# A WKV recurrence on one core: another order of the small state work and of the first loads

## The chip, the cores and the metric

The kernel runs on one core of a Trainium2 chip. A core has a matrix engine (PE, TensorE), a vector engine (DVE, VectorE), a scalar engine (ACT, ScalarE) and a general engine (POOL, GpSimd); SP (SyncE) here only issues transfers. Each engine takes its own instructions strictly in order and waits for the others through semaphores. Sixteen DMA engines move data between the chip's memory (HBM) and the core; the transfers that POOL issues stand under q0 in the profile, those of SP under q1. The metric is the device time of one launch in microseconds (us): the median of the executions shown.

## The reference

For each of 16 sequences and each of 256 channels, a running sum with exponential weights over 2048 tokens, kept safe by a running maximum `pp`:

```python
for b in range(batch):                 # 16
    aa, bb, pp = zeros, zeros, full(-1e38)
    for t in range(seq_len):           # 2048
        kk, vv = k[b, t, :], v[b, t, :]
        ww = u + kk
        qq = maximum(pp, ww)
        e1, e2 = exp(pp - qq), exp(ww - qq)
        output[b, t, :] = (e1 * aa + e2 * vv) / (e1 * bb + e2 + 1e-08)
        ww = pp - w + kk
        qq = maximum(ww, kk)
        e1, e2 = exp(ww - qq), exp(kk - qq)
        aa, bb, pp = e1 * aa + e2 * vv, e1 * bb + e2, qq
```

`k`, `v` and the output are 16 x 2048 x 256 in float32, 33.6 MB each; `w` and `u` are rows of 256.

## The kernel before

**Tiling.** The 2048 tokens are cut into a head of 32 (`T0`) and 16 steps of 126 (`TC`). Tokens lie on partitions. A step is worked on in four pairs, each with four sequences (a tile of 128 x 1024 float32, 512 KB, for `k` and one for `v`; the rows beyond 126 belong to the next step). The head fills two pairs of its own, three groups of 32 tokens stacked on 96 partitions, loaded by small transfers, one for each group. All pairs stand in one list: step 0's first two, the two head pairs (numbers 2 and 3), step 0's last two (4 and 5), then four for each step; 66 in all.

**One pair.** `round_k` (DVE, L287) casts `k` into a tile `km` that also holds `w` and `u` in its last rows; `logs` (PE, L303) multiplies it by two constant matrices into `X`, four PSUM banks (all the log weights); `exps` (ACT, L319; L317 in two parts for pairs 0 to 7) makes `ez` of it; `cast_v` (L330 on DVE, L328 on ACT for pairs 2 to 7) and `times_v` (DVE, L338) multiply by `v`; `sums` (PE, L368) adds up the pair's tokens into the step's totals `tot`. Ten slots later (`LAG`; six for a head pair) the pair's output is made: `den` (PE, L514), its logarithm `log_den` (ACT, L523), `invert` one slot later (ACT, L528), and in the slot after that `num` (PE, L536), `mult` (DVE, L544) and `store` (POOL, L564), `num` and `mult` once for each half of the pair. `den` has one PSUM buffer and `num` has one: `num` of the second half cannot start before `mult` of the first half has read the buffer.

**The state.** Between steps a small state is carried: `copy_sums` (ACT) takes the totals, `turn_sums` (PE, L384) transposes them into the buffer of `den`, `split_sums` (DVE, L391, tile `tsum`) takes them from there, and then a dozen instructions on tiles of some 64 columns follow, DVE and ACT by turns: `state_logs`, `state_offset` (tile `S`, L408), `state_near` (L412), `state_weights`, `state_sums` (`tb`, L441), `state_add` (`da`, L446), `state_decay` (`AB`, L452), `inject_logs`, `inject_weights` (`phi`), `carry_weights` (L468), `carries` (`ab`, L475), `turn_carries` (PE, L481, also in the buffer of `den`), and `inject` (DVE, `row`, L486), which ends in four small transfers on SP's queue (L490) that put the carried state into two rows of `ez`. The `den` of the step's pairs needs those rows.

**Order.** One loop (L617 to L674) runs over slots n; slot n works on `exps`, `times_v` and `sums` of pair n, on `round_k`, `cast_v` and `logs` of pair n+1, on the loads of pair n+4 and on the output of older pairs. The order of the calls is kept on every engine, so a call's place in the loop is its place in its engine's queue. The state's work is hung into the loop by name: `small_work(n, "d0")` and so on run what `PLANS` has put there, as (slots after the step's last pair, place, function). The first letter of a place says which engine it is meant for: d for DVE, p for PE, a for ACT. In slot 10 alone (`late`) `den` and `log_den` stand behind `sums`.

**Loads.** Four buffers for each of `k` and `v`. Pairs 0 to 3 are loaded ahead of the loop: the rows of `w` and `u`, then the two first pairs, and then the head's ten small transfers, all on SP's queue; all later loads and the stores are issued by POOL, in order. POOL also makes constant patterns; those for the head (`patterns_for_head`) come after the head's loads, and DVE makes matrices of them (`matrices_for_head`) after the first pair's casts.

Of the kernel before, what the change touches and what calls it, by code (L numbers as in the profile page):

```python
# [22 lines left out]
def kernel(  # L23
# [90 lines left out]
    def load(n):  # L114
        kr = kpool.tile([128, 4, Dm], F32, tag="kr", name="kr")
        vr = vpool.tile([128, 4, Dm], F32, tag="vr", name="vr")
        kr_of[n], vr_of[n] = kr, vr
        c, p = pairs[n]
        if is_head(n):
            if p == 1:  # L120
                K(POOL.memset(kr[64:96, 0:2, :], 0.0))
                K(POOL.memset(vr[64:96, 0:2, :], 0.0))
            for t, x in ((kr, k), (vr, v)):
                for g in range(NG):
                    b = 6 * g + 4 * p
                    e = min(b + 2 * tiles_of(n), B)
                    if b < e:
                        K(SP.dma_start(out=t[g * GB:(g + 1) * GB, 0:e - b, :],
                                        in_=x[b:e, 0:T0, :].rearrange("n t d -> t n d")))
        else:  # L130
            t0 = T0 + c * TC
            r = min(128, T - t0)
            for t, x in ((kr, k), (vr, v)):
                K((SP if n < 2 else POOL).dma_start(  # L134
                    out=t[0:r, :, :], in_=x[4 * p:4 * p + 4, t0:t0 + r, :].rearrange("n t d -> t n d")))
# [71 lines left out]
    K(DVE.scalar_tensor_tensor(NLE[:, TC + 1:128], cc[:, 2:3], -0.5 * HS, cc[:, 4:5], ALU.mult, ALU.add))  # L207
    for n in range(2, AHEAD):
        load(n)
# [8 lines left out]

    OHE, OHV, OHhE, OHhV = [matrix(x, BF16, 56) for x in ("OHE", "OHV", "OHhE", "OHhV")]

# [7 lines left out]

    def patterns_for_head():
        unit(0, NH)  # L230
        unit(1, NH + 1)
        K(POOL.iota(IOh[:, 0:NH], pattern=[[0, NG], [1, GB]], base=0, channel_multiplier=0,
                    allow_small_or_imprecise_dtypes=True))
        K(POOL.memset(OHhE, 0.0))
        K(POOL.memset(OHhV, 0.0))
        for g in range(NG):
            K(POOL.memset(OHhE[g * GB:(g + 1) * GB, 8 + 3 * g:9 + 3 * g], 1.0))
            K(POOL.memset(OHhV[g * GB:(g + 1) * GB, 24 + 3 * g:25 + 3 * g], 1.0))
            select(OHhE[:, 40 + 3 * g:41 + 3 * g], NE, 1.0, NH + g, -1, 1, 0)
# [117 lines left out]
    def sums(n):  # L357
# [5 lines left out]
        for i in range(tiles_of(n)):  # L363
            for q in range(2):
# [211 lines left out]
    def small_work(n, where):  # L576
        for f, args in later.pop((n, where), []):
# [3 lines left out]
        "head": ((1, "a0", copy_sums), (1, "p2", turn_sums), (2, "d0", split_sums), (2, "a1", state_logs),  # L581
                 (3, "a0", state_weights), (3, "d4", state_start)),
# [26 lines left out]
    patterns_for_head()  # L609
# [4 lines left out]
    matrices_for_head()  # L614

    out_at = {n + (LAG - 4 if is_head(n) else LAG): n for n in range(NP)}
    for n in range(NP + LAG + 2):  # L617
# [5 lines left out]
        if n + AHEAD < NP:  # L623
            load(n + AHEAD)
        if live:
            exps(n)
# [14 lines left out]

        late = n == LAG
        if out_q and not late:
# [7 lines left out]
        if out_qp:  # L651
            mult(qp, 0)
            if live:
                num(qp, 1)
# [18 lines left out]
        small_work(n, "d5")  # L673
        small_work(n, "a1")  # L674
# [31 lines left out]
```

## Time and profile before

| what | value |
|---|---|
| median of 13 runs | 331.9 us (325.75 to 337.45) |
| the profiled execution | 331.9 us, of it 330.2 us from its first to its last instruction |
| HBM read and written | 68.10 MB and 34.05 MB |
| POOL issues of loads and stores of 512 KB | 60 stores, 58 loads of `k`, 58 of `v`; median 7.5, 8.3 and 8.7 us from issue to landing |
| state transfers on SP's queue (`ez<-row`) | 64 of 8 KB, median 6.6 us to landing |
| mean granted PE clock | 0.965 of full speed |

By stages, as the stretches of the trace show them: up to about 44 us the pipeline fills (pairs 0 to 9, the head among them); up to about 94 us the first outputs begin; from 94.4 to 285.7 us eleven steps run alike, four pairs in about 17.4 us each; after 291 us the outputs of the last pairs are finished, with one logarithm and one exponential on ACT for each pair, about 2 us.

How to read the lines that follow. A line of busy time gives us and the share of the span for each engine. The rows of digits cut the span into 40 equal slices: a digit is a busy share in tenths. A line of the waits names the engine and line that waited, what it waited for, and then us in total, times, and the longest. A line of the timeline gives start, duration, engine, line, operation and shapes; in brackets stand the engine's idle time before it and what ended that. A line of stretches gives, for each, the busy us of each engine, the granted PE clock, the busy share of the DMA engines and GB/s.

### The profile page before, as it was taken

How to read it: one execution, taken by the hardware profiler on the slowest of the kernel's cores; microseconds unless marked ns; L12 is line 12 of the kernel's file. 1: busy time of each engine (PE TensorE's matmuls, PEld its weight loads, DVE VectorE, ACT ScalarE, POOL GpSimd, SP SyncE). 2: the span in 40 equal slices, each digit the busy share in tenths (PEclk: the TensorE clock that was granted, in tenths of full speed). 3: DMA queues.
4: the chain of work that ended last, by engine and by line, in shares of the span. 5: the costliest groups of instructions: out<-in, count | busy, mean ns of one | idle time of the engine just before them, and what ended most of it. 6: DMA issues, size and time to landing. Idle time of an engine off the chain costs nothing.

```text
span 330.2 us, 3900 instructions
## 1 busy us (share of the span) xinstructions
PE 282.9 (86%) x1116; PEld 130.4 (39%) x1132; DVE 275.7 (84%) x547; ACT 280.5 (85%) x318; POOL 176.0 (53%) x244
## 2 busy tenths in 40 slices
PE   1649795979999999999999999999999999997980
PEld 1214332434444444444444444444444444433430
DVE  4824794697999999999999999999999999997761
ACT  6439784859989898999999998999898989897890
POOL 7328963336446566656555666666564656111431
PEclk9996989599999999999999999999999999999996
DMA  5997699849999999999999999999999999954776
GB/s 174 284 288 247 186 324 325 240 145 329 325 334 355 350 356 357 379 368 354 368 370 378 357 361 370 378 348 355 360 375 362 365 330 323 299 217 134 257 264 180
DMA packets 34071, 102.93 MB, mean 312 GB/s; under 512 B 6610, under 2 KB 9938, under 8 KB 34050
## 3 DMA queue, kind: packets, MB, share of 16 engines
q0 software_dynamic: 27408, 98.75, 87.4%
q1 hardware_dynamic: 6642, 3.94, 4.8%
q8 instruction: 9, 0.15, 0.2%
q14 instruction: 12, 0.10, 0.1%
HBM read 68.10 MB, written 34.05 MB: 309 GB/s over the span
## 4 chain that ended last, share of the span: by engine, by line
PE 37%; DMA 25%; DVE 20%; ACT 10%; issue 5%; SPq 1%; DVEq 0%; POOL 0%; POOLq 0%; ACTq 0%
DMA vr<-in_v_dram 21%; PE num L536 10%; PE tot L368 9%; PE X L303 8%; DVE rd L544 6%; PE den L514 6%; DVE ez L338 5%; DMA ez<-row 5%; DVE vb L330 3%; ACT rd L523 3%; DVE km L287 3%; ACT ez L317 2%; ACT ez L319 2%; PE den L384 2%; ACT vb L328 1%
## 5 line engine op out<-in xcount | busy, mean ns | idle before, releaser
L319 ACT ACTIVATE ez<-X 128x2048 bf16<-128x2048 f32 x58 | 108.8, 1876 | 15.5 <-PE X L303 15.2
L564 POOL DMA_DIRECT2D out_dram<-rd x64 | 50.0, 781 | 120.0 <-issue 76.4
L544 DVE TENSOR_TENSOR rd<-num,rd 128x512 f32<-128x512 f32 (+2 forms) x131 | 88.5, 682 | 9.1 <-ACT rd L528 5.1
L338 DVE TENSOR_TENSOR ez<-ez,vb 126x2048 bf16<-126x2048 bf16 (+1 forms) x66 | 79.8, 1209 | 4.2 <-ACT ez L317 4.1
L523 ACT ACTIVATE rd<-den 128x1024 f32<-128x1024 f32 (+3 forms) x67 | 66.4, 991 | 7.2 <-PE den L514 7.2
L528 ACT ACTIVATE rd<-rd 128x1024 f32<-128x1024 f32 (+3 forms) x67 | 68.9, 1028 | 0.3
L134 POOL DMA_DIRECT2D kr<-in_k_dram x62 | 60.4, 974 | 9.1 <-DVE km L287 4.2
L303 PE MATMUL X<-km,NLE 128*128 128x512 f32 x128 | 53.9, 503 | 12.3 <-DVE km L287 11.1
L536 PE MATMUL num<-ez,LfN 128*128 128x512 bf16 x128 | 48.7, 380 | 8.3 <-DVE rd L544 7.6
L134 POOL DMA_DIRECT2D vr<-in_v_dram x62 | 50.9, 820 | 8.3 <-ACT vb L328 6.6
L368 PE MATMUL tot<-ez,OHE 128*48 128x512 bf16 x128 | 51.1, 399 | 0.0
L368 PE MATMUL tot<-ez,OHV 126*48 126x512 bf16 x128 | 49.8, 389 | 0.9 <-DVE ez L338 0.7
L536 PE MATMUL num<-ez,IdN 126*128 126x512 bf16 (+1 forms) x131 | 50.0, 382 | 0.0
L287 DVE CAST km<-kr 126x1024 fp32r<-126x1024 f32 x64 | 44.5, 696 | 1.3 <-DMA kr<-in_k_dram 1.3
L330 DVE CAST vb<-vr 126x1024 bf16<-126x1024 f32 x60 | 42.4, 707 | 1.7 <-DMA vr<-in_v_dram 1.7
L303 PE MATMUL X<-km,NLZ 128*128 128x512 f32 x128 | 42.3, 413 | 0.0
L514 PE MATMUL den<-ez,Id 126*128 126x512 bf16 (+1 forms) x131 | 39.5, 382 | 0.9
L514 PE MATMUL den<-ez,Lf 128*128 128x512 bf16 x112 | 35.0, 382 | 4.4 <-DMA ez<-row 1.6
L303 PEld LDWEIGHTS X<-km,NLE 128*128 128x128 f32 x128 | 24.7, 200 | 24.4 <-DVE km L287 7.2
L303 PEld LDWEIGHTS X<-km,NLZ 128*128 128x128 f32 x128 | 25.5, 200 | 6.3 <-ACT ez L317 0.4
L368 PEld LDWEIGHTS <-OHE 128*48 128x48 bf16 x128 | 13.1, 102 | 35.5 <-issue 33.2
L536 PEld LDWEIGHTS <-IdN 126*128 126x128 bf16 (+1 forms) x131 | 12.7, 97 | 25.3 <-issue 21.8
(111 smaller groups left out, 215.2 us busy)
## 6 DMA issues: line engine op xcount, KB each, us to landing
out_dram<-rd POOLq DMA_DIRECT2D x60, 512.0 KB, 7.5
kr<-in_k_dram POOLq DMA_DIRECT2D x58, 512.0 KB, 8.3
vr<-in_v_dram POOLq DMA_DIRECT2D x58, 512.0 KB, 8.7
kr<-in_k_dram POOLq DMA_DIRECT2D x4, 504.0 KB, 9.8
vr<-in_v_dram POOLq DMA_DIRECT2D x4, 504.0 KB, 10.9
out_dram<-rd POOLq DMA_DIRECT2D x3, 504.0 KB, 4.3
kr<-in_k_dram SPq DMA_DIRECT2D x2, 512.0 KB, 5.0
vr<-in_v_dram SPq DMA_DIRECT2D x2, 512.0 KB, 6.6
```

The source lines that it names most:

```text
L134: K((SP if n < 2 else POOL).dma_start(out=t[0:r, :, :], in_=x[4 * p:4 * p + 4, t0:t0 + r, :].rearrange("n t d -> t n d")))
L287: K(DVE.tensor_copy(KM[n][0:r, 0:i, :], kr_of.pop(n)[0:r, 0:i, :]))
L303: K(PE.matmul(X[q][:, i, :], m[0:kr, :], km[0:kr, i, :], start=True, stop=True))
L319: K(SC.activation(ez_of(n)[:, 0:4:2], X[2][:, :, 0:i, :], ACT.Exp))
L330: K(DVE.tensor_copy(vb[0:r, 0:i, :], vr_of.pop(n)[0:r, 0:i, :]))
L338: K(DVE.tensor_mul(ez[0:r, 1:4:2], ez[0:r, 0:4:2], vb[0:r, 0:i, :].unsqueeze(1).broadcast_to([r, 2, i, D])))
L368: K(PE.matmul(TOT[c], m[0:r, :], ez_of(n)[0:r, q, i, :], start=n == first_of[c] and i == 0 and q == 0, stop=n == last_of[c] and i == tiles ...
L514: K(PE.matmul(d[:, i, :], m[0:r, :], ez_of(n)[0:r, q, i, :], start=q == 0, stop=q == 2, skip_group_check=True))
L523: K(SC.activation(RD[n][0:r, a:b, :], DEN[n][0:r, a:b, :], ACT.Ln, scale=RS))
L528: K(SC.activation(RD[n][0:r, a:b, :], RD[n][0:r, a:b, :], ACT.Exp, scale=-1.0))
L536: K(PE.matmul(d, m[0:r, :], ez_of(n)[0:r, q, i, :], start=q == 1, stop=q == 3, skip_group_check=True))
L544: K(DVE.tensor_mul(RD[n][0:r, i, :], NUM.pop((n, i))[0:r, :], RD[n][0:r, i, :]))
```

## The change

It moves instructions; beside the rows of `w` and `u` and one memset it adds and removes none.

- `w` and `u` are each read into 16 rows of `crow` (before: 2 rows each, the other 28 rows zeroed by a DVE memset); `w` on SP's queue, `u` on ACT's.
- The head's `k` transfers stay on SP's queue; its `v` transfers go to POOL's, last group first. POOL's head patterns come ahead of the head's loads.
- `matrices_for_head` moves from the end of the preparation to place d1 of slot 0, behind `round_k` of pair 1 and `cast_v` of pair 0.
- In every slot with output, `logs` of the next pair is called ahead of `num` of the second half (before: behind it). The special case of slot 10 is gone.
- `sums` does the two matmuls with exponentials (`OHE`) first and then the two with products (`OHV`); before, the two kinds took turns.
- The plans for the state: in steps 1 to 14 ("steady") no two of its instructions on DVE stand in one place, and only `inject` follows directly on another one, `carries`; `split_sums` comes behind `round_k`; step 0's plan ("first") ends one slot earlier. New places: a3, a4, p3, p4.

```diff
-            for t, x in ((kr, k), (vr, v)):
-                for g in range(NG):
+            for t, x, eng, groups in ((kr, k, SP, range(NG)), (vr, v, POOL, reversed(range(NG)))):
+                for g in groups:
...
-                        K(SP.dma_start(out=t[g * GB:(g + 1) * GB, 0:e - b, :],
+                        K(eng.dma_start(out=t[g * GB:(g + 1) * GB, 0:e - b, :],
...
-    K(DVE.memset(crow[96:128, :], 0.0))
-    for r, x in ((96, w), (97, u)):
-        K(SP.dma_start(out=crow[r:r + 31:30, :], in_=bass.AP(
-            tensor=x.tensor, offset=x.offset, ap=[[0, 2], list(x.ap[0])])))
+    for r, x, eng in ((96, w, SP), (97, u, SC)):
+        K(eng.dma_start(out=crow[r:128:2, :], in_=bass.AP(
+            tensor=x.tensor, offset=x.offset, ap=[[0, 16], list(x.ap[0])])))
...
+    unit(0, NH)
+    unit(1, NH + 1)
+    K(POOL.iota(IOh[:, 0:NH], pattern=[[0, NG], [1, GB]], base=0, channel_multiplier=0,
...
     for n in range(2, AHEAD):
         load(n)
...
-        for i in range(tiles_of(n)):
-            for q in range(2):
+        for q in range(2):
+            for i in range(tiles_of(n)):
...
-        "first": ((1, "a0", copy_sums), (1, "p2", turn_sums), (2, "d0", split_sums), (2, "a0", state_logs),
-                  (2, "d4", state_offset, 0), (2, "d4", state_offset, 1), (2, "d4", state_near),
-                  (2, "a1", state_weights), (3, "d0", state_sums), (3, "d0", state_add, 0),
-                  (3, "d1", state_decay, 0), (3, "a0", inject_logs), (3, "a1", inject_weights),
-                  (4, "d0", carry_weights), (4, "d0", carries), (4, "p0", turn_carries), (4, "d1", inject),
-                  (4, "d4", state_add, 1), (4, "d5", state_decay, 1)),
-        "steady": ((1, "a0", copy_sums), (1, "p2", turn_sums), (2, "d0", split_sums), (2, "a0", state_logs),
-                   (2, "d4", state_offset, 0), (2, "d5", state_offset, 1), (3, "d0", state_near),
-                   (3, "a0", state_weights), (3, "d4", state_sums), (3, "d5", state_add, 0),
-                   (4, "d0", state_decay, 0), (4, "a0", inject_logs), (4, "a0", inject_weights),
-                   (4, "d5", carry_weights), (5, "d0", carries), (5, "p0", turn_carries), (5, "d1", inject),
-                   (5, "d4", state_add, 1), (5, "d5", state_decay, 1)),
+        "first": ((1, "a0", copy_sums), (1, "p3", turn_sums), (1, "d5", split_sums), (1, "a1", state_logs),
+                  (2, "d1", state_offset, 0), (2, "d1", state_offset, 1), (2, "d1", state_near),
+                  (2, "a0", state_weights), (2, "d3", state_sums), (2, "d3", state_add, 0),
+                  (2, "d3", state_decay, 0), (2, "a1", inject_logs), (2, "a1", inject_weights),
+                  (3, "d0", carry_weights), (3, "d0", carries), (3, "p0", turn_carries), (3, "d1", inject),
+                  (3, "d4", state_add, 1), (3, "d5", state_decay, 1)),
+        "steady": ((1, "a0", copy_sums), (1, "p2", turn_sums), (2, "d1", split_sums), (2, "a2", state_logs),
+                   (2, "d3", state_offset, 0), (2, "d4", state_offset, 1), (2, "d5", state_near),
+                   (3, "a0", state_weights), (3, "d2", state_sums), (3, "d3", state_add, 0),
+                   (3, "d4", state_decay, 0), (4, "a0", inject_logs), (4, "a2", inject_weights),
+                   (4, "d4", carry_weights), (4, "d5", carries), (4, "p4", turn_carries), (5, "d0", inject),
+                   (5, "d2", state_add, 1), (5, "d4", state_decay, 1)),
...
+    at(0, "d1", matrices_for_head)
...
-    patterns_for_head()
...
-    matrices_for_head()
...
+        small_work(n, "a3")
         if live:
             exps(n)
...
-        late = n == LAG
-        if out_q and not late:
+        if out_q:
             den(q)
...
         if out_qp:
             mult(qp, 0)
-            if live:
-                num(qp, 1)
         small_work(n, "d2")
         if more:
             cast_v(n + 1)
         small_work(n, "d3")
+        small_work(n, "a4")
         if more:
             logs(n + 1)
+        if live and out_qp:
+            num(qp, 1)
+        small_work(n, "p3")
         if live:
             times_v(n)
-        if live:
             sums(n)
-        if late:
-            den(q)
-            log_den(q)
         small_work(n, "p2")
         small_work(n, "d4")
         if out_qp:
             mult(qp, 1)
             store(qp)
         small_work(n, "d5")
+        small_work(n, "p4")
         small_work(n, "a1")
```

More of the change, by code (lines that the diff above doesn't have):

```diff
@@ L207 @@
     K(DVE.scalar_tensor_tensor(NLE[:, TC + 1:128], cc[:, 2:3], -0.5 * HS, cc[:, 4:5], ALU.mult, ALU.add))
+    OHE, OHV, OHhE, OHhV = [matrix(x, BF16, 56) for x in ("OHE", "OHV", "OHhE", "OHhV")]
+    unit(0, NH)
+    unit(1, NH + 1)
+    K(POOL.iota(IOh[:, 0:NH], pattern=[[0, NG], [1, GB]], base=0, channel_multiplier=0,
+                allow_small_or_imprecise_dtypes=True))
+    K(POOL.memset(OHhE, 0.0))
+    K(POOL.memset(OHhV, 0.0))
+    for g in range(NG):
+        K(POOL.memset(OHhE[g * GB:(g + 1) * GB, 8 + 3 * g:9 + 3 * g], 1.0))
+        K(POOL.memset(OHhV[g * GB:(g + 1) * GB, 24 + 3 * g:25 + 3 * g], 1.0))
+        select(OHhE[:, 40 + 3 * g:41 + 3 * g], NE, 1.0, NH + g, -1, 1, 0)
     for n in range(2, AHEAD):
@@ L216 @@
         K(SC.activation(t[96:98, :, :], row_of(96, 98), ACT.Copy))
-    OHE, OHV, OHhE, OHhV = [matrix(x, BF16, 56) for x in ("OHE", "OHV", "OHhE", "OHhV")]
     def matrices_for_sums():
@@ L227, in matrices_for_sums @@
         K(DVE.tensor_copy(OHE[:, 40:49:8], cc[:, 2:4]))
[L229 to L239, printed above, removed]
     def matrices_for_head():
@@ L580 @@
     PLANS = {
-        "head": ((1, "a0", copy_sums), (1, "p2", turn_sums), (2, "d0", split_sums), (2, "a1", state_logs),
+        "head": ((1, "a0", copy_sums), (1, "p2", turn_sums), (2, "d1", split_sums), (2, "a1", state_logs),
                  (3, "a0", state_weights), (3, "d4", state_start)),
-        "first": ((1, "a0", copy_sums), (1, "p2", turn_sums), (2, "d0", split_sums), (2, "a0", state_logs),
-                  (2, "d4", state_offset, 0), (2, "d4", state_offset, 1), (2, "d4", state_near),
-                  (2, "a1", state_weights), (3, "d0", state_sums), (3, "d0", state_add, 0),
-                  (3, "d1", state_decay, 0), (3, "a0", inject_logs), (3, "a1", inject_weights),
-                  (4, "d0", carry_weights), (4, "d0", carries), (4, "p0", turn_carries), (4, "d1", inject),
-                  (4, "d4", state_add, 1), (4, "d5", state_decay, 1)),
```

## The prediction

> **What bounds the kernel now.** First the page: the busy shares, then the rows of slices, then the list of waits for what is left.
>
> ```profile
> PE 282.9 (86%) x1116; PEld 130.4 (39%) x1132; DVE 275.7 (84%) x547; ACT 280.5 (85%) x318; POOL 176.0 (53%) x244
> DVE  4824794697999999999999999999999999997761
> DMA  5997699849999999999999999999999999954776
> GB/s 174 284 288 247 186 324 325 240 145 329 325 334 355 350 356 357 379 368 354 368 370 378 357 361 370 378 348 355 360 375 362 365 330 323 299 217 134 257 264 180
> ```
>
> Four resources stand at or near nine tenths from 90 to 290 us, so no one engine is "the" bound; what a change can earn there is a few per cent. The holes are in the first 80 us and the last 40.
>
> The stretches give one of the eleven like steps (198.7 to 216.1 us, 17.4 us):
>
> ```profile
> 198.70:216.10 17.40, 16.42 (x69) 7.63 (x69) 16.56 (x34) 16.38 (x19) 9.95 (x12) 1.00 1.02 375
> ```
>
> In order: PE, PEld, DVE, ACT, POOL, clock, DMA share, GB/s. DVE is idle 0.84 us of it, the least. The waits say on what:
>
> ```profile
> DVE tsum L391 <- PE den L384: 17.4, 16, 4.9
> PE num L536 <- DVE rd L544: 8.4, 27, 1.1
> ACT rd L523 <- PE den L514: 7.2, 5, 4.4
> DVE kmh L287 <- DMA kr<-in_k_dram: 6.1, 1, 6.1
> ACT vb L328 <- DMA vr<-in_v_dram: 5.2, 1, 5.2
> ```
>
> DVE waits once a step for the transposed totals: 0.65 us in a regular step, the rest (4.9, 1.9, 1.4, 1.3) early. The last two rows are the head's data. Why they come late is seen in the queues between 14 and 22 us:
>
> ```profile
> q0 software_dynamic: 616, 2.26, 89.0%
> q1 hardware_dynamic: 378, 0.31, 14.9%
> ```
>
> (packets, MB, share of the 16 engines.) From 6 to 8 us q1 alone moved 0.71 MB. Once POOL's loads of pairs 4 and 5 run, SP's queue gets 0.31 MB in 8 us, and the head's second half of `k` and most of its `v` are in it. The third hole, in the timeline:
>
> ```profile
> 55.51 0.38 PE L514 MATMUL den<-ez,Lf 128*128 128x512 bf16 x1 [1.40 <-DMA ez<-row]
> 56.57 1.02 ACT L523 ACTIVATE rd<-den 128x1024 f32<-128x1024 f32 x1 [4.44 <-PE den L514]
> 58.73 0.36 DVE L391 COPY tsum<-den 128x192 f32<-128x192 f32 x1 [4.89 <-PE den L384]
> ```
>
> The first `den` waits for step 0's state rows, issued at 47.59; ACT and DVE stand behind it.
>
> **The change, part by part** (against the profiled execution: 330.2 us of span, 1.7 around it; its 331.9 equals the median).
>
> *Head.* (a) The DVE memset ahead of the first transfer and the issue of `u` (0.60 us on SP's queue) go; the first `k` is issued at about 1.65 instead of 2.67 and SP's queue runs 1 us earlier. ACT pays an issue of about 0.6 us ahead of its table load (1.28 us), ready at 2.7, while its copies of `crow` started at 3.91: covered. (b) The matrices for the head, 2.35 us of DVE (8.82 to 11.17), went ahead of the cast of pair 1, whose `k` had landed at about 10.0; now behind it, so pair 1's `logs` start near 9.9 instead of 12.01. `cast_v` of pair 1 and `times_v` of pair 0 stand behind the matrices now; the first comes near 12.1, before 12.80 (its `v` landed at about 12.8, 1 us earlier by part a). (c) SP's queue carries 2.6 instead of 3.15 MB (four transfers of 524288 bytes and the head's 0.52 MB of `k`), and at the 0.31 to 0.35 MB per us that it had alone from 4 us on it is empty near 11 us, before POOL's traffic starts (the first q0 packets came at about 13). The head's `v` is first in POOL's queue: at 0.3 MB per us, 0.5 MB lands near 13; before, ACT got the first half at 20.39. (d) Price: POOL's head patterns, 1.9 us, and five issues of 0.56 (the row of the head's stores, 1.66 for three) stand ahead of pair 4's loads, which go out near 10 instead of 7.45; they land near 15 and 17 and are needed at 18 and 20. Pair 4's `exps`, at 27.20 before, follows DVE, PE and ACT work without a wait at 21 to 22. I take 5.5 us; bounds 1 (only part a) and 7.
>
> A rule speaks against (c). The POOL row: 62 issues of `v`, 748 to 1203 ns with median 751, many beside DVE casts. The Trainium skill, "SBUF — State Buffer", section "SBUF: two separate sides", says that POOL cannot write descriptors while DVE runs a float32 copy within SBUF; the section after it ("A bandwidth-pool intuition that's wrong (but worth ruling out)") puts a 620 ns transfer at about 3100 ns beside one. By the page five issues would be 15.5 us, the head's `v` land after 22 us, and the head earn nothing: the sum below would be -6. By the row they cost 2.8, at worst 6. I take the row.
>
> *First state, slot 10.* `inject` of step 0 moves from slot 9 to slot 8. Counted from the same start, DVE reaches it at about 44.1 instead of 47.21, behind casts at 43.35 and the two small carries. Landing took 7.9 us (47.59 to about 55.4), so the rows are there at 52. `den` now stands ahead of `logs` in slot 10, wants to start at 49.5 and waits 2 to 2.5 us with `logs` of pair 11 queued behind it; then `exps` of pair 11 can start near 54 instead of 57.49. ACT pays in slot 6: `state_logs` now stands in front of `exps` of pair 7 and waits for `tsum`, 0.9 us. Its four issues on SP's queue (2.49 us) have nothing behind them. Net 3 us; bounds 1 and 4.5.
>
> *Steady steps.* (e) `split_sums` behind `round_k` (0.60 from start to start) gives the totals that time, and `sums` with its products last frees PE about 0.2 us earlier: the 0.65 goes. Next late is `num`, behind `turn_sums` (0.56 on PE): some 0.2 remains. (f) A small DVE instruction that needs the one just before it costs more: S to `near` 0.22 from start to start, `da` to `AB` 0.31, `phi` to `ab` 0.24, against 0.10 to 0.13 for S or `da` ahead of other work. All three pairs are pulled apart: 0.4. (g) Against it, `row` now stands directly behind `ab`, with PE between them:
>
> ```profile
> 210.71 0.29 DVE L475 TENSOR_TENSOR ab<-AB,phi 128x128 bf16<-128x128 f32 x1
> 210.92 0.69 DVE L287 CAST km<-kr 126x1024 fp32r<-126x1024 f32 x1
> 211.52 0.28 DVE L486 CAST row<-den 128x128 bf16<-128x128 f32 x1
> ```
>
> PE's turn starts at 211.06 and takes 0.23; `row` can start at about 211.4, so DVE, free at 210.92, loses 0.45, and `round_k` and `mult` behind it move with it. (h) `logs` ahead of the second `num`: PE no longer idles for `mult` (8.4 us in all), but `num` comes about 1.2 us later. In the slot at 220 us `den` ends its issue at 221.49, `logs` would take 1.22, `num` be ready at 223.3; DVE reaches the second `mult` at 223.20, and at 223.0 in slots without a small instruction: 0.1 to 0.3 late in two slots of four, say 0.2 a step. Sum a step: -0.65 + 0.2 - 0.4 + 0.45 + 0.2 = -0.2; `exps` earlier (ACT waits 15.2 us for `X` in all, 0.65 in the slot of `tsum`) and `den` no longer waiting for `row` (0.3 to 0.57 of PE) give PE and ACT back about 0.2, a part of which DVE feels. On ACT `state_logs` and `inject_weights` (0.26 and 0.35) step behind an `invert` of 1.05; what DVE makes of them stands three places or a slot later, so they cost nothing, and 0.3 a step if DVE should come first. I take -0.35, times eleven: -4; bounds -0.8 and +0.4 a step.
>
> *DMA.* A step moves 12 transfers of 524288 bytes, 6.29 MB, 362 GB/s at 17.4 us. The Trainium skill ("DMA: Bandwidth & Descriptors", "Specifications") sets about 358 GB/s for one core's HBM; by that a step needs 17.6 us and (e) to (h) earn nothing. The rows show 375 over a whole step and 379 in a slice, which allow 16.6 to 16.8. I take the rows. But near the end the `v` of pair 65 was already waited for (DVE, 0.9 us), at 311 GB/s from 268 on; a faster step exposes that: +1, bounds 0 and 3.
>
> Sum: -5.5 - 3 - 4 + 1 = -11.5. The last 40 us, bound by ACT's 2 us a pair, keep their work. 331.9 - 11.5 = 320.4: 320.
>
> **The rivals.** (1) *DMA is the floor from 90 to 290 us.* For: its share is 1.00 or more in every step. Against: only one wait for a load there, at its end; 375 GB/s in some steps. Then loads become late a few slots after the gain, steady steps stay at 17.4, and some of the head's gain is given back: -5.5 - 3 + 2 = -6.5, 325.
> (2) *Slower: the second `num` behind `logs`.* One mechanism: in slots 12 to 65 DVE finds `num` unready at its second `mult`. The other gains come to about 11.5; over 54 pairs that is 0.21 us a pair, the point from which it decides. `logs` takes 1.22 of PE, and cover is `cast_v` and `times_v`, 1.74; if PE runs 0.4 later against DVE than in the slot at 220, the price is 21.6 and the time 342. For: PE is at 16.4 of 17.4 too. Against: PE leads at `times_v` by its two exponential `sums`.
> (3) *The steady part does not do what it says*: `row` behind `ab` and waits for PE cost what `tsum` gave, and the first state moves its wait into slot 10: -5.5 - 1 + 1.5 = -5, 327.
>
> **How the numbers follow.** Forecast 0.50 (312 to 323), DMA floor 0.22 (323 to 327), steady lost 0.12 (325 to 330), head lost as well (328 to 334) 0.07, slower by (2) 0.09. The range 312 to 330 leaves out (2), half of the head lost and under 0.05 below 312. About 1% (3.3 us) is what a measurement of this kernel can tell from no change: faster 0.83 (forecast, floor, 0.10 of the steady lost, 0.01 of the head lost), same 0.08, slower 0.09.
>
> **What would show it.** Head: no wait of DVE or ACT for the head's `kr` and `vr` over 1 us, pair 4's `exps` near 21 to 22. First state: `ez<-row` issued some 9 us earlier than 47.6, its wait at the first `den` about 2 us, DVE's 4.9 gone. Steady: the wait of `tsum` under 0.2, new waits of `row` for `turn_carries` of about 0.45 and of the second `mult` for `num`; `near`, `AB` and `ab` not behind their sources; a step of 17.0. Wrong would be: steps of 17.4 with waits for `kr` or `vr` (1), or `mult` waiting 0.2 and more in each slot (2).

## The result, and the profile after

| | before | after |
|---|---|---|
| median | 331.9 us (48 runs) | 326.3 us (321.44 to 328.42, 11 runs) |
| ratio to before | | 0.9865, 95% interval [0.9812, 0.9918] |
| profiled span | 330.2 us | 322.0 us |

Faster by 5.6 us in the medians, where 11.5 were forecast; the ratio, which compares only the faster executions of each kernel with one another, says 4.5 us. First the page of the kernel after: the busy shares, and the rows of slices for DVE, the DMA engines and what they moved.

```profile
PE 277.9 (86%) x1115; PEld 125.7 (39%) x1132; DVE 278.0 (86%) x546; ACT 278.2 (86%) x318; POOL 179.6 (56%) x249
...
DVE  4857857989999999999999999999999999877660
...
DMA  6999798999999999999999999999999999954975
GB/s 204 253 349 348 228 340 222 321 348 322 346 347 350 368 365 363 360 365 355 361 365 371 363 357 369 357 358 352 375 367 364 367 290 289 292 188 135 303 252 162
```

The start moves more data in its first slices. The hole of before near 70 us (145 GB/s) is gone; a shallower one, 222 GB/s, stands near 52 us. In the middle little has changed: from about 100 to 258 us the slices move 350 to 375 GB/s, before 348 to 379. The waits of after (engine and line, what it waited for, us in all, times, longest):

```profile
DVE row L484 <- PE den L479: 4.5, 14, 0.3
DVE rd L542 <- PE num L534: 4.5, 6, 2.6
...
DVE km L285 <- DMA kr<-in_k_dram: 2.6, 4, 0.9
...
PE den L512 <- DMA ez<-row: 2.2, 1, 2.2
...
DVE vb L328 <- DMA vr<-in_v_dram: 1.9, 3, 1.0
...
DVE tsum L389 <- PE den L382: 1.3, 3, 0.5
...
PE num L534 <- DVE rd L542: 0.8, 1, 0.8
```

The 17.4 us of `tsum` have become 1.3, and `row` waits 0.3 in 14 steps. `mult` waits for `num` six times only, not in every slot. Yet one step, with the same columns as before:

```profile
190.14:207.60 17.46, 16.44 (x70) 7.55 (x70) 16.76 (x33) 16.15 (x18) 10.19 (x13) 1.00 1.02 364
```

takes 17.46 us where before took 17.40, and DVE, third of the busy columns, is busy 16.76 us in it instead of 16.56, although its instructions are the same. So a wait was taken away from DVE and its work grew.

Two executions of each kernel, cut at the start of `exps` of certain pairs (the second is the same kernel in a later run, below), in us. The forecast for the ten steps is -0.35 a step, ten times:

| from, to (start of `exps`) | before | after | mean difference | forecast |
|---|---|---|---|---|
| start, pair 10 | 49.27, 46.42 | 41.68, 45.97 | -4.0 | -5.5 |
| pair 10, 20 | 48.13, 47.63 | 45.25, 42.82 | -3.8 | -3 |
| pair 20, 60 (ten steps) | 173.86, 173.97 | 174.59, 174.63 | +0.7 | -3.5 |
| pair 60, 65 | 21.38, 21.39 | 22.90, 23.18 | +1.7 | +1 |
| pair 65, end | 37.53, 37.54 | 37.57, 39.02 | +0.8 | 0 |

The steady part is where the forecast gain is missing; the start differs by several us between two executions of one kernel. The experiments follow both.

### The profile page after: what moved, and what is told of

Its sections match the earlier page's. It is cut to its first block, busy times and chain, and to the rows that moved or that the text cites. A ratio compares the mean times of both kernels' runs of the same rounds, so it can differ in the third digit from the quotient of the medians.

```text
span 322.0 us, 3957 instructions
## 1 busy us (share of the span) xinstructions
PE 277.9 (86%) x1115; PEld 125.7 (39%) x1132; DVE 278.0 (86%) x546; ACT 278.2 (86%) x318; POOL 179.6 (56%) x249
## 5 line engine op out<-in xcount | busy, mean ns | idle before, releaser
L562 POOL DMA_DIRECT2D out_dram<-rd x64 | 54.1, 846 | 120.6 <-issue 45.4
L521 ACT ACTIVATE rd<-den 128x1024 f32<-128x1024 f32 (+3 forms) x67 | 67.0, 999 | 17.4 <-PE den L512 15.1
L301 PE MATMUL X<-km,NLE 128*128 128x512 f32 x128 | 52.5, 492 | 10.7 <-DVE km L285 7.1
L135 POOL DMA_DIRECT2D kr<-in_k_dram x62 | 55.9, 902 | 0.4 <-issue 0.4
L135 POOL DMA_DIRECT2D vr<-in_v_dram x62 | 49.2, 793 | 2.9 <-ACT vb L326 2.1
L328 DVE CAST vb<-vr 126x1024 bf16<-126x1024 f32 x60 | 46.5, 774 | 1.9 <-DMA vr<-in_v_dram 1.9
L366 PE MATMUL tot<-ez,OHV 126*48 126x512 bf16 x128 | 38.8, 385 | 8.3 <-DVE ez L336 6.9
L301 PE MATMUL X<-km,NLZ 128*128 128x512 f32 x128 | 41.4, 405 | 0.3 <-ACT ez L315 0.3
L366 PE MATMUL tot<-ez,OHE 128*48 128x512 bf16 x128 | 40.1, 395 | 0.0
L366 PEld LDWEIGHTS <-OHV 126*48 126x48 bf16 x128 | 13.4, 104 | 30.6 <-issue 21.6
L534 PEld LDWEIGHTS <-LfN 128*128 128x128 bf16 x128 | 12.3, 96 | 28.6 <-issue 25.4
```

The source lines that it names most:

```text
L135: K((SP if n < 2 else POOL).dma_start(out=t[0:r, :, :], in_=x[4 * p:4 * p + 4, t0:t0 + r, :].rearrange("n t d -> t n d")))
L301: K(PE.matmul(X[q][:, i, :], m[0:kr, :], km[0:kr, i, :], start=True, stop=True))
L328: K(DVE.tensor_copy(vb[0:r, 0:i, :], vr_of.pop(n)[0:r, 0:i, :]))
L366: K(PE.matmul(TOT[c], m[0:r, :], ez_of(n)[0:r, q, i, :], start=n == first_of[c] and i == 0 and q == 0, stop=n == last_of[c] and i == tiles ...
L521: K(SC.activation(RD[n][0:r, a:b, :], DEN[n][0:r, a:b, :], ACT.Ln, scale=RS))
L534: K(PE.matmul(d, m[0:r, :], ez_of(n)[0:r, q, i, :], start=q == 1, stop=q == 3, skip_group_check=True))
```

## Experiments

"Step" below is a tenth of the time from the cast of `k` (`round_k`) of pair 20 to that of pair 60 in the profiled execution, within 0.015 us of what the start of `exps` gives; "cast" is the mean in us of the 40 casts of `v` of the pairs 20 to 59. Each ratio is to before, run beside it on the same chip, with its 95% interval.

**The same kernels again.** No edit.

> The kernel before, once more, for a second profile of it. The times of single executions differ by some 3%, the profiled one of before had a span of 330.2 us and that of the change 322.0, while the ratio of the times is 0.9865 (4.5 us). If the difference sits in the fill or in the clock of single executions, this span is 326 to 328 with pair 12's cast near 55 to 57 instead of 59.0 and steady steps of 17.39 again; if the steps differ between executions, they are 17.2 here.

> The changed kernel once more, beside the three that follow and the kernel before, on one chip. Cast theory: its steady step is 17.4 to 17.5 us again and 20 of the 40 casts of v take 0.88 to 0.92 us. Ratio to before 0.980 to 0.992. The chain of the head (first exps of the fourth pair) began at 21.1 us in the first profile; if that is an event of single executions it lies anywhere in 20 to 25 here; if it belongs to the changed start it is 21 again.

Before: 0.9992 [0.9943, 1.0042], step 17.385, cast 0.700 us. After: 0.9818 [0.9724, 0.9913], step 17.462, cast 0.796 us, and again 20 of the 40 casts over 0.8 us. The steps repeat within 0.01 us; the start does not: `exps` of pair 4 began at 27.20 and 23.35 in before, at 21.09 and 24.48 in after.

**One part undone or alone.** Before's steady plan in the changed kernel; `logs` of the changed kernel put behind the second `num` again; the start of the changed kernel alone, in before.

```diff
-        "steady": ((1, "a0", copy_sums), (1, "p2", turn_sums), (2, "d1", split_sums), (2, "a2", state_logs),
...
+        "steady": ((1, "a0", copy_sums), (1, "p2", turn_sums), (2, "d0", split_sums), (2, "a0", state_logs),
...
```

> The changed kernel with the steady plan of before. Gap theory: from the second mult of a pair to the first of the next there is a chain mult, num, mult of 1.42 us (num has one buffer) beside 1.2 us of DVE's own work, and small instructions put into that gap cost nothing; the changed plan took most of them out. Then this kernel's step is 17.0 to 17.3 and it is 2 to 4 us faster than the changed one (ratio to before about 0.975). Port theory: the step is 17.45 because two casts of v a step are stretched by 0.22 when they begin in the middle of POOL's issue of k; the plan decides that only by the phase. DMA theory: every order gives 17.4 to 17.5, ratio 0.987.

```diff
-        if more:
-            logs(n + 1)
         if live and out_qp:
             num(qp, 1)
+        if more:
+            logs(n + 1)
```

> The changed kernel with logs behind the second num again. If logs ahead is what takes PE's waits away, PE waits for mult again (8 us in all) and the step grows by 0 to 0.3 us (ratio to before 0.987 to 0.998). Gap theory: no change of the step within 0.1, since DVE's gaps stay as they are. DMA theory: 17.4 to 17.5 again.

> The kernel before with only the start changed: rows of w and u on two queues, the head's v from POOL, patterns ahead of the loads, head matrices in slot 0. By the prediction pair 4's exps comes 5.5 to 6.1 us earlier (27.2 to about 21.1) and the whole is 5 to 6 us faster (ratio 0.982 to 0.985), with steps of 17.39. If the loads then catch up with the DMA engines, half of it is lost by slot 20 and the ratio is 0.99 or above.

| | ratio | step | cast, and how many over 0.8 us |
|---|---|---|---|
| before's steady plan | 0.9905 [0.9853, 0.9957] | 17.447 | 0.700, 1 |
| `logs` behind `num` | 0.9869 [0.9827, 0.9910] | 17.464 | 0.797, 20 |
| new start alone | 1.0000 [0.9952, 1.0048] | 17.485 | 0.700, 1 |

The place of `logs` is worth nothing in either direction: rival 2 is out, and so is the 0.2 a step charged for it. The long casts come with the new plan and go with the old one. The step stays at 17.45 all the same, because the old plan brings its waits for `tsum` back (11.2 us in all, against 1.3), so this run alone does not say what the casts cost. The start alone earned nothing that the median shows, though pair 10 came at 45.07.

**Why half of the casts are long.** First the casts of `v` (minimum, median and maximum in ns) between 94 and 285 us; before, in its second execution:

```profile
L330 DVE CAST vb<-vr x44: 675/684/839, 96.4 to 283.7; 126x1024 bf16<-126x1024 f32 x44
```

and after:

```profile
L328 DVE CAST vb<-vr x44: 681/688/1009, 93.6 to 282.2; 126x1024 bf16<-126x1024 f32 x44
```

The median hides it, the timeline of after shows it:

```profile
207.05 0.75 POOL L135 DMA_DIRECT2D kr<-in_k_dram  x1
...
207.42 0.90 DVE L328 CAST vb<-vr 126x1024 bf16<-126x1024 f32 x1
...
207.79 0.83 POOL L135 DMA_DIRECT2D vr<-in_v_dram  x1
...
211.57 1.16 POOL L135 DMA_DIRECT2D kr<-in_k_dram  x1
...
211.74 0.69 DVE L328 CAST vb<-vr 126x1024 bf16<-126x1024 f32 x1
...
213.75 0.68 DVE L542 TENSOR_TENSOR rd<-num,rd 128x512 f32<-128x512 f32 x1
...
214.35 0.68 DVE L285 CAST km<-kr 126x1024 fp32r<-126x1024 f32 x1
...
214.48 0.38 PE L534 MATMUL num<-ez,LfN 128*128 128x512 bf16 x1
...
215.17 0.69 DVE L542 TENSOR_TENSOR rd<-num,rd 128x512 f32<-128x512 f32 x1
```

A cast that begins 0.37 us into POOL's issue of `kr` takes 0.90 us and the issue is as short as ever; one that begins 0.17 us into it takes 0.69, and the issue is the long one, 1.16. POOL has time (10 of 17.4 us busy), DVE has not. In the changed kernel two of four slots have the first phase. In before none has: one of its four casts begins 0.53 us into the issue and takes 0.74 us, the others begin in the first 0.23 us of an issue.

All 20 profiles of the study agree, for the casts of `v` of the pairs 20 to 59 that begin within an issue of `kr`. The 338 that begin in its first quarter of a microsecond take 0.67 to 0.72 us, and the issue ends 0.98 to 1.03 us after the start of the cast. Of the 234 that begin 0.3 to 0.6 us into it, 210 end 1.25 to 1.29 us after the start of the issue, whenever they began, and 21 more up to 0.1 us later. By an estimate from these figures POOL holds such a cast up until about 0.59 us into its issue (1.27 less the 0.68 of a free cast), and no longer.

To move the phase, five memsets of one column were put on POOL ahead of each pair's two loads, from the load of pair 16 on (0.23 to 0.78 us of POOL ahead of a pair of loads):

```diff
+            if n >= LAG + AHEAD + 2:
+                for j in range(PAD):
+                    K(POOL.memset(pad[:, j:j + 1], 0.0))
             for t, x in ((kr, k), (vr, v)):
```

> The changed kernel with five tiny memsets on POOL ahead of each pair's loads from pair 16 on, which start POOL's issue of k about 0.25 us later against DVE. Port theory: the cast of v then begins in the first 0.2 us of the issue, DVE is not held and POOL is; the long casts (20 of 41, 0.90 us) go back to 0.68 and the step falls by up to 0.4, to 17.1. Gap and DMA theories: the casts may change, the step stays at 17.4 to 17.5, because DVE then waits for num or for loads instead.

0.9590 [0.9512, 0.9669], 317.4 us. The casts of `v` here:

```profile
L334 DVE CAST vb<-vr x43: 681/684/778, 96.7 to 275.8; 126x1024 bf16<-126x1024 f32 x43
```

and in the timeline POOL is the one that pays:

```profile
202.94 0.23 POOL L139 MEMSET pad<- 128x1 f32 x5
...
203.08 1.21 POOL L141 DMA_DIRECT2D kr<-in_k_dram  x1
...
203.31 0.68 DVE L334 CAST vb<-vr 126x1024 bf16<-126x1024 f32 x1
```

The step is 17.094: 0.37 shorter than in the changed kernel, for 40 casts that are 0.093 us shorter in the mean (0.703), 0.37 us for the four of a step. Work added to an engine off the path made half of the casts of the engine on it 0.22 us shorter. As a control, the memsets behind the two loads:

> The control to the pad: the same five memsets on POOL from pair 16 on, but behind the two loads, so that the start of POOL's issue of k does not move against DVE. Port theory: 20 of 40 casts of v stay at 0.90 and the step at 17.4 to 17.5, ratio to before 0.987 as for the changed kernel. If the memsets help in some other way (pace of the queue, fewer transfers at once), the step is 17.1 as with the pad ahead.

```profile
L334 DVE CAST vb<-vr x43: 681/724/1007, 95.5 to 278.9; 126x1024 bf16<-126x1024 f32 x43
```

Step 17.487, cast 0.804, 20 long: the steady part is that of the changed kernel, so the position counts. Its total, 0.9608 [0.9557, 0.9660], is nevertheless low. Its profile has pair 10 at 41.13, pair 60 to 65 in 21.27 instead of 22.9; so the spacing of POOL's issues probably helps the end, and the rest is the start, which the memsets did not cause: the first of them runs at 54.4 us. The two totals alone would not have told the two versions apart.

To see how much the transfers themselves cost, the changed kernel with two of the four sequences of each pair's output not stored (except in the very last pair):

> The changed kernel storing only the first two of each pair's four sequences (pairs of the steps; half of the output is left out, all arithmetic stays). Traffic of a step falls by a sixth, from 6.29 to 5.24 MB. DMA theory: the step falls below 17.2, towards what PE, DVE and ACT need (16.7 or less). Gap and port theories: the step stays at 17.4 to 17.5 while the DMA share falls to about 0.85 and transfers land 2 us sooner; only the last step, where loads were late, gains 1 us.

0.9624 [0.9525, 0.9724], step 17.029, cast 0.684. This edit moved POOL against DVE as well, and the casts became short. A sixth of a step's bytes taken away earns only 0.07 us a step against the version with memsets ahead, and the casts, 0.019 us shorter than there, would give as much: at 17.1 us the DMA engines were not what held it.

**The gap.** `num` has one buffer. From the second `mult` of a pair to the first of the next, `num` must be made in between: above, 213.75 to 215.17, 1.42 us, with a single cast in it that ends at about 214.95. Before had small instructions there:

```profile
219.12 0.68 DVE L544 TENSOR_TENSOR rd<-num,rd 128x512 f32<-128x512 f32 x1
219.72 0.18 DVE L408 SCALAR_TENSOR_TENSOR S<-S,lf 128x32 f32<-128x32 f32 x1
219.94 0.21 DVE L412 TENSOR_SCALAR near<-S 128x96 f32<-128x96 f32 x1
220.06 0.69 DVE L287 CAST km<-kr 126x1024 fp32r<-126x1024 f32 x1
220.66 0.68 DVE L544 TENSOR_TENSOR rd<-num,rd 128x512 f32<-128x512 f32 x1
```

Two of them, 1.54 us in all: 0.12 more than the empty gap. In the mean of ten steps, the change shortened the four gaps of a step by 0.97 us (7.54 to 6.57) and lengthened the other halves of the pairs by 1.05 (9.85 to 10.90). The long casts are in those halves: with the memsets ahead of the loads they are 10.49, so 0.64 is left. Instructions went from where they were nearly free to where they are paid in full. The plan that puts them back, still never two that depend on each other in a row:

```diff
+        "steady": ((1, "a0", copy_sums), (1, "p2", turn_sums), (2, "d1", split_sums), (2, "a2", state_logs),
+                   (2, "d4", state_offset, 0), (2, "d5", state_offset, 1), (3, "d1", state_near),
+                   (3, "a2", state_weights), (3, "d4", state_sums), (3, "d5", state_add, 0),
+                   (4, "d1", state_decay, 0), (4, "a2", inject_logs), (4, "a2", inject_weights),
+                   (4, "d4", carry_weights), (4, "d5", carries), (4, "p4", turn_carries), (5, "d1", inject),
+                   (5, "d1", state_add, 1), (5, "d5", state_decay, 1)),
```

> The changed kernel with another steady plan: most of the state's small DVE instructions sit between the second mult of a pair and the first of the next (places d5 and d1), split_sums and inject behind round_k, only offset 0, sums and carry_weights elsewhere. Gap theory: the step falls by 0.4 to 0.7 us, to about 16.9, and the whole by 5 to 7 us (ratio to the changed kernel 0.98). DMA theory: the step stays at 17.3 to 17.5, and waits of casts for kr or vr appear in its place, or transfers land later. Port theory: the step moves only as far as the long casts of v (0.90 against 0.68) come or go.

0.9756 [0.9676, 0.9837]. Four steps of 16.65 us, then, from about 150 us, 16.9 to 17.5, and a last steady step of 21.9. Again, on another chip:

> The gap plan without the pad again. Its first profile went from 16.65 us a step to 17.3 and a late last step, with landings at 11 us. Theory A (the pad spares the drift: without it casts and loads collide once the step is at 16.7): it drifts again, landings of 10 us and more, and its median lies 5 us or more above that of the gap plan with the pad. Theory B (the drift was the DMA rate of one execution or chip): no drift here, 16.7 to the end, landings near 8, and the two medians lie within 2 us.

0.9815 [0.9724, 0.9906]; five steps of 16.5 to 16.7, then 17.2 to 17.4, and 22.7. The drift is not the casts: in the six drifting steps of the first run none of `v` takes over 0.8 us. POOL now waits for the transfers that it issued before; the waits:

```profile
POOL vr L135 <- DMA out_dram<-rd: 13.4, 23, 1.1
...
ACT rd L521 <- DMA out_dram<-rd: 12.7, 16, 2.7
...
POOL kr L135 <- DMA vr<-in_v_dram: 11.1, 24, 1.6
```

and transfers land later, as its list of issues has them (KB each, median us to landing):

```profile
out_dram<-rd POOLq DMA_DIRECT2D x60, 512.0 KB, 9.2
kr<-in_k_dram POOLq DMA_DIRECT2D x58, 512.0 KB, 9.8
vr<-in_v_dram POOLq DMA_DIRECT2D x58, 512.0 KB, 10.5
```

That looked like the DMA floor of rival 1. Three versions of this plan say otherwise: half of the stores left out as above, the memsets ahead of the loads, and the memsets behind them.

> The gap plan with only the first two of each pair's four sequences stored (half of the output of the steps is left out). With all stores its steps took 16.65 us four times and then 17.2 to 17.3, with transfers landing after 11 us. DMA theory for that drift: with 5.24 MB a step it stays at 16.6 to 16.7 to the end and landings stay under 8 us. If the drift is something else (phase of DVE and POOL, PE), it comes back.

> The gap plan with the pad ahead of the loads. DMA theory: the gap plan already stands at the floor that the DMA engines set (17.2 to 17.3 once eight transfers are out at a time), so nothing comes on top: steps 16.6 to 16.8 at first, 17.0 to 17.3 later, and the ratio to before is no better than the pad's alone, 0.959. If the drift came from the port, steps stay at 16.65 and the ratio is 0.95 or less.

> The gap plan with five small memsets of POOL ahead of each pair's loads, again. Cast and gap theories together: step 16.7 to the end, casts of v at 0.70, landings near 8 us, ratio to before 0.925 to 0.945, some 14 to 17 us below the changed kernel of this call. If the DMA were the limit at 17 us a step, it would drift like the gap plan's first run and end within 8 us of the changed kernel.

> The gap plan with the five memsets behind each pair's two loads instead of ahead of them. It tells what ended the drift of the gap plan (landings of 11 us from the ninth step on, steps of 17.2 and a last step of 22). If the drift came from DVE casts that begin inside an issue, this version still drifts or has long casts of v (mean over 730 ns), and its time is 318 or more. If it came from POOL issuing its loads in one bunch with the next pair's, and any idle time between the pairs of loads cures it, landings stay near 8 us, the last step is under 17.2, and its time is within 3 us of the version with the memsets ahead (0.936 of before).

| gap plan with | ratio | median us | step | cast, over 0.8 us |
|---|---|---|---|---|
| half of the stores (two executions) | 0.9428 [0.9360, 0.9496] | 314.4 | 16.73 | 0.679, 0 |
| memsets ahead of the loads | 0.9322 [0.9265, 0.9379] | 310.2 | 16.70 | 0.696, 0 |
| the same again | 0.9356 [0.9267, 0.9444] | 311.2 | 16.69 | 0.695, 0 |
| memsets behind the loads | 0.9379 [0.9233, 0.9525] | 313.1 | 16.64 | 0.732, 8 |

None of the four drifts. With all of its traffic, the version with memsets ahead lands its stores in 7.3 and its loads in 7.9 and 8.2 us (second run):

```profile
out_dram<-rd POOLq DMA_DIRECT2D x60, 512.0 KB, 7.3
kr<-in_k_dram POOLq DMA_DIRECT2D x58, 512.0 KB, 7.9
vr<-in_v_dram POOLq DMA_DIRECT2D x58, 512.0 KB, 8.2
```

and two steps of its first run, as stretches, show 358 and 397 GB/s at 16.70 us:

```profile
182.50:199.20 16.70, 15.97 (x69) 7.52 (x69) 16.34 (x33) 16.15 (x19) 10.38 (x32) 1.00 1.00 358
199.20:215.90 16.70, 16.09 (x69) 7.38 (x69) 16.34 (x33) 16.14 (x19) 10.38 (x32) 1.00 1.02 397
```

A steady step of 16.70 with everything moved is 377 GB/s, so the drift at 17.2 was not the highest rate of the memory. The memsets need not stand ahead of the loads to end the drift; some time of POOL between one pair's transfers and the next is enough. What exactly queues up without it is open. So is what holds the step with the memsets behind: its eight long casts did not make it longer than with the memsets ahead. The gap in this version, in its timeline:

```profile
199.38 0.68 DVE L548 TENSOR_TENSOR rd<-num,rd 128x512 f32<-128x512 f32 x1
199.98 0.17 DVE L412 SCALAR_TENSOR_TENSOR S<-S,lf 128x32 f32<-128x32 f32 x1
200.08 0.68 DVE L291 CAST km<-kr 126x1024 fp32r<-126x1024 f32 x1
200.68 0.19 DVE L416 TENSOR_SCALAR near<-S 128x96 f32<-128x96 f32 x1
200.80 0.67 DVE L548 TENSOR_TENSOR rd<-num,rd 128x512 f32<-128x512 f32 x1
```

1.42 us with two state instructions in it, what the changed kernel takes with none. From the changed kernel with memsets (17.09) to this one it is 0.40 us a step: the gaps grew by 0.18 us (6.57 to 6.75) and the other halves shrank by 0.53 (10.49 to 9.96). This version is the best of all: 311.2 us beside 326.8 for the changed kernel and 330.8 for before on one chip.

**The first state.** Step 0's plan and slot 10 as before, the rest of the change kept.

```diff
+        late = n == LAG
+        if out_q and not late:
-        if out_q:
             den(q)
...
+        if late:
+            den(q)
+            log_den(q)
```

> The changed kernel with step 0's plan and slot 10 as before (den behind sums, inject in slot 9). By the prediction 3 us are lost (1 to 4.5): pair 12's cast comes 3 us later against pair 9's than in the changed kernel, and the ratio to before goes from 0.987 to about 0.995. If the early state is worth nothing, the ratio stays at 0.987.

0.9863 [0.9780, 0.9946]; pair 10 to 20 in 46.9 us. The total does not show a loss (the changed kernel had 0.9865 and 0.9818); its interval reaches 2.7 us to either side, so it does not exclude one either. Over all profiles of the study: 45.0 to 48.1, mean 47.1, in the five executions with before's order of the first state; 41.9 to 45.3, mean 43.6, in nine with the new one (leaving out those with the gap plan, whose steps differ). That is 3.5 us at pair 20. How much of it reaches the end is open.

**The start.** The changed kernel with before's start:

> The changed kernel with the start of before (rows of w and u, head loads on SP's queue alone, patterns and head matrices as before). By the prediction 5.5 us are lost (ratio to before 1.003). By the two looks at the kernel before (pair 4's exps at 27.2 and at 23.35, against 21.1 to 24.8 in seven kernels with the new start) the head's wait is an event of single executions: 0 to 3 us are lost in the median (ratio 0.987 to 0.996), and this profile shows pair 4's exps anywhere from 23 to 27.

> The changed kernel with the start of before, rows of w and u on one queue, head loads of v behind those of k on SP, small patterns ahead of the first scan. Theory that the start is worth what the prediction said: 4 to 7 us above the changed kernel's median in this call, and the fourth pair's exps later by as much. Rival (the head waits for a landing whose time differs by execution, whatever the order): within 2 us of the changed kernel, and the fourth pair's exps anywhere in 22 to 30 us. The step stays 17.4.

0.9831 [0.9753, 0.9908] and 0.9832 [0.9749, 0.9914]; the changed kernel beside the second had 0.9818, medians of 326.7 and 326.8 us. In the profiles `exps` of pair 10 began at 46.1 to 50.8 (mean 47.9, without the latest 47.2; five executions) with the old start and at 41.1 to 46.0 (mean 44.0, fifteen) with the new. So the start does come earlier, by 3 to 4 us in the mean. In the pair of runs on one chip 0.2 us is left at pair 20 (88.79 and 88.97) of 1.1 at pair 10: `den` of slot 10 waits 1.43 us for the state rows with the new start and 0.51 with the old. Over all profiles this wait does not follow the start (2.33 us in the one that starts latest), so what takes the gain from the medians is not shown. The start alone in before led its neighbour, the second execution of before, by 1.1 us at pair 20 and had lost it by pair 60.

The two runs with the old start also show the cost of a cast within one execution. Their steps take turns: those whose four casts of `v` sum to 3.15 to 3.17 us take 17.43 to 17.45, those with 3.06 to 3.09 take 17.34 to 17.37.

**A control that did not come out.** The memsets ahead of the loads in before, whose casts were short.

> The kernel before with the five memsets ahead of each pair's loads from pair 16 on. Control: its casts of v took 0.70 us already, so by the theory of casts stretched by POOL's issue there is nothing to cure: ratio 0.995 to 1.005, step 17.3 to 17.5. If the memsets helped by something else (the spacing of the transfers alone), it would be faster by 1% or more, with a step near 17.0.

0.9850 [0.9750, 0.9949], with a step of 17.512 and ten long casts. The steady part got no faster, by the theory of casts it had nothing to gain, and the new phase even made some casts long: four times the 0.035 us that the mean cast grew is the 0.13 that the step grew. The 1.5% lie elsewhere: its profile gained 3.1 us on the second execution of before by pair 12, whose `exps` began at 56.78 us, and its first memset at 57.0; there the state rows landed 5.9 to 6.6 us after their issue instead of 7.2 to 7.8. Whether that is chance or a place in memory that moved with the small new tile is open. A single total of this kernel within 1.5% of another should not be read as a cause.

## Why the prediction was right and wrong

The sign and the range were right, and so were the mechanisms that it saw. The size failed: of the forecast's -11 us in the table above -4.6 came, and 4.2 of the missing 6.4 lie in the steady term.

- *Steady steps, -4: the term that failed.* Parts (e) to (h), taken as -0.35 a step, hold when the phase is cleared: 17.094 against 17.385 is -0.29. Of them (e) is right (`tsum` waits 1.3 us in all), (g) was 0.32 instead of 0.45, (h) 0 instead of 0.2. What the sum put at nothing is the hold of POOL's issues on DVE: +0.37 a step for the casts of `v`. The working had the cause in hand: it weighed the rule of the Trainium skill, "SBUF — State Buffer", "SBUF: two separate sides", for POOL's five issues in the head, found POOL hardly delayed (by the issues of `v`, median 751 ns; those of `kr`, which meet the casts, take 974 in the mean on the page of before), and did not ask the reverse question, what an issue does to a cast that starts during it. That section says that the one that starts first keeps the port and the other fully blocks. The traces agree that one of the two waits and that DVE can be the one, but not for the whole of the other's instruction: a cast that starts 0.37 us into an issue pays 0.22 us, not the 0.38 that the issue still had to run; and 0.17 us into it POOL pays, though POOL was first. That the port is what they wait for is the page's account; the runs show the order and the cost.
- *Where a state instruction stands, (f) and the plan.* The forecast counted what dependent neighbours cost and not that the places d5, d0 and d1 lie in the time DVE spends waiting for `num`'s one buffer. With the casts cured, moving the instructions back there is worth another 0.40 a step, as long as the transfers keep up.
- *The head, -5.5.* -4.0 at pair 10 in two executions of each kernel, near 0 in the medians on one chip. The step that failed is the reading of one profile as the rule: in before's profiled execution the head's `v` landed at 20.3 us, in its second at 15.0, so part of the loss that (c) repaired was an event of that execution; and of 1.1 us on one chip slot 10 took back 0.9. The move itself did what was said: in after the head's `v` landed at 13.0 to 15.7 us. POOL's five issues took 3.7 us (2.47 for three, 1.24 for two), more than the 2.8 of the row and far from the 15.5 by the page: the row was the better guide there. Between 14 and 22 us of after SP's queue is empty (by (c) from near 11; from 12 to 14 it still moved 0.11 MB), and the packets are POOL's and one of instruction loading:

```profile
q0 software_dynamic: 703, 2.55, 102.0%
q14 instruction: 1, 0.01, 0.3%
```

- *The first state, -3.* Right at pair 20: 3.5 us, though the total of the run without it does not show them; and the wait moved to the first `den` as the working said, 2.2 us there and 2.47 behind it on ACT; the timeline of after:

```profile
45.33 0.38 PE L512 MATMUL den<-ez,Lf 128*128 128x512 bf16 x1 [2.21 <-DMA ez<-row]
...
47.01 1.02 ACT L521 ACTIVATE rd<-den 128x1024 f32<-128x1024 f32 x1 [2.47 <-PE den L512]
...
48.72 1.88 ACT L317 ACTIVATE ez<-X 128x2048 bf16<-128x2048 f32 x1 [0.68 <-PE X L301]
```

- *The end, +1.* Right in kind, 1.7 in size, and 0.8 more behind pair 65 that one of the two executions shows.
- *Rivals.* (1) gave nearly the right number, 325, for a wrong reason: the steps stayed at 17.4 with no wait of DVE for a load between pairs 20 and 60, and 16.70 us a step was reached with all of the traffic. (2) was out. (3) was nearest to what happened, steady part lost, but not through `row` and PE: through a longer instruction, which no list of waits shows.

## What to carry to other kernels

When DVE is the bound and POOL issues the transfers, look at the durations of one kind of DVE instruction one by one, not at their median, and against POOL's timeline; a shift of either engine by a few tenths of a microsecond costs or saves a third of a cast. Put small instructions into the stretch that an engine must wait through anyway (here the turn of a single buffer), and count a moved instruction by the place it leaves as well as the place it takes. Take the start of a kernel from several executions before giving it a number.

## What the runs showed of the hardware

- A DVE cast of 126 x 1024 float32 that begins some 0.37 us into a POOL issue of 0.75 us takes 0.90 us instead of 0.68; begun 0.17 to 0.23 us into it, it keeps 0.68 and the issue takes 1.16 to 1.21. Begun anywhere from 0.3 to 0.6 us into it, the cast ends some 1.27 us after the start of the issue.
- Steps moved 6.29 MB in 16.70 us, 377 GB/s for ten steps in a row, with single steps at 397; the section "Specifications" of "DMA: Bandwidth & Descriptors", with about 358 GB/s for a core's memory, would have put the step at 17.6.
- In the gap plan, five memsets on POOL ahead of each pair's loads made the transfers of the same bytes land after 7.3 to 8.2 us instead of 9.2 to 10.5, and the kernel 13 us shorter (two runs on one chip).
- With the new start the steady step was 0.05 to 0.1 us longer than with the old (17.462 and 17.409 for the changed kernel, 17.485 and 17.385 for before), with the same instructions. In the changed kernel the casts account for it: 0.796 against 0.782 us, 0.06 for four. In before they do not (0.700 both times): half of it is one single step of 17.99, and the rest is open.
